# Values and gates of a gated recurrence as one block product in seven parts

## The chip, the cores and the metric

The kernel runs on one core of a Trainium2 chip. Its engines are named as in the profile: PE multiplies matrices (its weight loads are shown apart, as PEld), DVE, ACT and POOL do vector and scalar work, and SP only issues transfers. Times are microseconds of device time; a kernel's time is the median of its runs, and less is better. "Product" below means one matrix instruction of PE.

## The reference

One layer of a streaming encoder, in float32, for 512 tokens of width 1024. The change is in the combined input projection and in what follows from two of its eight outputs, `gi` (the recurrence's values) and `gg` (its gates):

```python
hn = rmsnorm(h, norm_mix_g[l])
proj = hn @ w_in[l]
fq, fk, fv, ff, gq, gf, gi, gg = jnp.split(proj, split_idx, axis=-1)
log_f = jax.nn.log_sigmoid((ff + fox_f_bias[l]).astype(jnp.float32)).transpose(0, 2, 1)
fox_out = fox_attention(to_heads(fq), to_heads(fk), to_heads(fv), log_f)
rec = hgrn2_chunkwise(gq, gf, gi, lbs[l])
rec = rmsnorm(rec, hgrn_norm_g[l]) * jax.nn.silu(gg...)
h = h + jnp.concatenate([fox_out, rec], axis=-1) @ w_out[l]
h = h + memory_cross_attention(rmsnorm(h, norm_x_g[l]), mem_n, ...)
h = h + jnp.square(jax.nn.relu(rmsnorm(h, norm_ff_g[l]) @ w1[l])) @ w2[l]
```

`w_in` has 3592 columns. `fv` is columns 1024 to 1535, `ff` 1536 to 1543, `gi` 2568 to 3079 and `gg` 3080 to 3591. `hgrn2_chunkwise` has 4 heads; in each chunk of 64 tokens its attention weights hold the product of the forget gates between two tokens, and a state of 128 x 128 per head goes from chunk to chunk.

## The kernel before, in words

**Products.** Every float32 operand is split into a high and a low part, and a matrix product is done as three: high by high, high by low, low by high. Tokens are contracted over 8 slices of 128 of the width; the scale of the norm (`r0`, one number per token) is applied to the result. `hn_hi` and `hn_lo` hold the transposed, gain-scaled input in its two parts; `x_T` makes them slice by slice, and `x_park` keeps the transposed input (`park`) and sends it to DRAM for the end of the layer.

**Weights.** They come as a stream of panels, in the order of the list `specs`. Each panel is two units (a and b, four slices of the width each, or two for wide panels of 512 columns). A unit is loaded by a transfer on SP into a `wr` tile (two buffers), ACT rounds it to its high part `wh` (L179), and DVE subtracts to get its low part `wl` (L183); four buffers hold the parts, two panels. `next_panel` hands out a panel and starts those up to two ahead, at a low priority. In this stretch the panels are: 0 and 1 the forget gates, 2 and 3 the queries of the recurrence (`gq`), 4 the first 256 columns of `gi` with the 8 of `ff`, 5 and 6 the two halves of the width for all of `gg`, 7 and 8 the same for the other 256 columns of `gi` with the first 256 of `fv`, and from 9 on the attention's queries and keys.

**The order.** PE's instructions run in the order in which the code writes them. The other engines' order is set by a scheduler from priorities. Between the steps of the recurrence the code puts products from a queue called `fill`: `fill.run(us)` takes products until their estimated time is used up, so PE has work while the vector engines do theirs.

**Levels.** The weights inside chunks are built in seven levels, m = 1, 2, 4 ... 64. A level is one set of products `lv` on PE from the tiles `mov` (keys and queries multiplied up) and `mix` (copies of them by ACT); DVE copies their results under a mask (L806); DVE and POOL multiply `mov` and `sta` by the gates' products `F` (DVE L825, POOL L826 for every other head), POOL multiplies `F` up (L828), ACT makes the next `mix`, and `fill.run(2 * F2)` follows. Level m = 64 instead puts its result into the tiles `A`. Then come the transposes of `A` (`pa`), the transposes of the keys (`pk`, copied by DVE to `kt` at L920), and the loop over the chunks with `po` and the state's product `pst` (L940), which reads `kt` and the values.

**Around it.** SP's queue also carries plain copies of MLP weights to DRAM (a table, `COPIES`, says how many after which load), on which POOL's accumulating transfers (L444) later add other blocks, at times given by `PACE`. The first row tile of the memory is loaded and normalised (L377 to L387) beside the keys.

Of the kernel before, what the change touches and what calls it, by code (L numbers as in the profile page):

```python
# [33 lines left out]
MT, NF = 3, 2  # L34
F1, F2, F3, F4, B1 = 1.6, 2.7, 1.5, 1.0, 2.0

# [4 lines left out]
RAWS, HB, LOADS = 5, 4, 8  # L41
COPIES = {7: 2, 16: 1, 17: 0, 21: 1}
PACE = (183.0, 4.7), (306.0, 11.5)


@with_exitstack
def emit(
# [141 lines left out]
    def load_unit(name, spec, ks, parts=1, between=None):  # L189
# [24 lines left out]
    def load_next(parts=2, between=None):  # L214

        i = len(stream)
        if i >= len(specs):
            return []
        units, splits = [], []
        uk = specs[i][0][1].shape[1] // 2  # L220
# [5 lines left out]
        stream.append(tuple([u[x] for u in units] for x in range(2)))  # L226
        return splits

    def next_panel():
# [179 lines left out]


    hn_hi, hn_lo = act_tile("hn_hi"), act_tile("hn_lo")
    xTd = drp.tile([4, P, 2, S], F32, name="xTd")
# [73 lines left out]
    presum.jobs.extend(j for _, j in sets)  # L486
    park = {}

# [18 lines left out]
    def x_park(c):  # L507
        part, new_ = c // 2, c // 2 not in park
        if new_:
            park[part] = s4([2, S], f"xT{part}")  # L510
        dst = park[part][:, c % 2, :]
# [4 lines left out]
        if not new_:  # L516
            gp.dma_start(xTd[part], park[part])

# [133 lines left out]
    gate(3)  # L652
    forget(3)
    for hp in range(2):
        wt = next_panel()
        for j in range(2):
            h = 2 * hp + j
# [32 lines left out]

    def proj_if():
        wt = next_panel()
        for tb in range(NT):
            ps = mm(f"gi0{tb}", (WT + FH,))
            yield from gemm_tm(ps, wt, hn_hi, hn_lo, tb)
            ac.activation(iv[tb // 2][:, tb % 2, 0:WT], ps[:, 0:WT], AF.Identity, scale=r0[:, tb : tb + 1])
            ve.scalar_tensor_tensor(z3[:, tb, :], ps[:, WT : WT + FH], r0[:, tb : tb + 1], fb, op0=ALU.mult, op1=ALU.add)
# [5 lines left out]

    fill.add(proj_if(), "ff")
    fill.add(new(gg, "gg"))
    fill.add(proj_wide([lambda tb: gg[tb // 2][:, tb % 2, :]], AF.Silu, "gg"), "gg")

# [4 lines left out]

    def proj_iv():
        yield from proj_wide([lambda tb: iv[tb // 2][:, tb % 2, WT:S], new_fv()], AF.Identity, "gi")

    fill.add(proj_iv(), "iv")

# [183 lines left out]

    mx_hi, mx_lo = act_tile("mx_hi"), act_tile("mx_lo")
    St = None
# [1015 lines left out]
```

## Time and profile before

| | |
|---|---|
| runs, us | 751.37, 751.83, 751.97 |
| median of the runs, us | 751.83 |
| the profiled execution, us | 751.99 |
| its span in the profile, us | 750.3 |
| mean granted clock of PE | 0.998 |
| bytes moved by transfers | 152.92 MB, 204 GB/s over the span |
| read from device memory, written | 147.91 MB, 51.40 MB |

The profile is of one execution. Rows that begin with a time are of the timeline: the start, how long, the engine, the code's line, the operation, what it writes and reads, the shape, and how many stand together; in brackets is how long the engine had been idle before and what it waited for last. Matrix instructions are pipelined and their ends are modelled, so starts are compared, not ends. Rows with a line first are groups: count, busy time and mean in ns, then idle time before them. Rows of transfers give their number, their size, and the median time from issue to landing.

### The profile page before, as it was taken

To read this page: it belongs to the slowest core of one execution; us is meant where nothing else is said; L and a number is where in the kernel's file an instruction comes from. 1 tells how busy PE (TensorE), PEld (TensorE's weight loads), DVE (VectorE), ACT (ScalarE), POOL (GpSimd) and SP (SyncE) were. 2 spreads that over 40 slices of the span, in tenths; PEclk is the share of its full clock that TensorE was granted. 3 is DMA by queue.
4 is the path that set the end of the run, shared out by engine and by line. 5 is a ranking of instruction groups with operands and counts; after the bars stand their busy time and mean duration, and the time that the engine had idled before them with its cause. 6 is when DMAs were issued, how large, how long until landed. Compare 5 with 4: busy or idle time off the path is not lost.

```text
span 750.3 us, 12293 instructions
## 1 busy us (share of the span) xinstructions
PE 742.9 (99%) x4581; PEld 649.6 (87%) x4581; DVE 546.5 (73%) x869; ACT 444.7 (59%) x749; POOL 202.1 (27%) x280
## 2 busy tenths in 40 slices
PE   9999999999999999999999999999999999999996
PEld 6889888888888888888888899898989899999985
DVE  5647873667878856645556898978787887878796
ACT  5655555556666742344434589666566757574864
POOL 7207531233433237621111212111111111100034
PEclk9999999999999999999999999999999999999999
DMA  8641987578957889985579799898989898978452
GB/s 250 200 116 58 298 262 228 172 231 269 289 187 224 265 225 210 193 165 122 121 165 197 114 250 238 237 226 247 230 218 235 220 247 214 240 198 232 133 113 113
DMA packets 109678, 152.92 MB, mean 204 GB/s; under 512 B 6145, under 2 KB 76074, under 8 KB 109618
## 3 DMA queue, kind: packets, MB, share of 16 engines
q1 hardware_dynamic: 85458, 112.52, 46.3%
q0 software_dynamic: 24000, 39.35, 30.1%
q8 instruction: 36, 0.59, 0.3%
q14 instruction: 24, 0.20, 0.1%
q10 hardware_dynamic: 160, 0.27, 0.1%
HBM read 147.91 MB, written 51.40 MB: 266 GB/s over the span
## 4 chain that ended last, share of the span: by engine, by line
PE 96%; DVE 1%; issue 1%; ACT 0%; POOL 0%; POOLq 0%; DVEq 0%
PE uU L1494 4%; PE uU L1496 4%; PE uU L1495 4%; PE U L1652 3%; PE U L1653 3%; PE U L1654 3%; PE uY L1495 2%; PE uY L1494 2%; PE uY L1496 2%; PE xk L1008 2%; PE xq L253 2%; PE wo L253 2%; PE xq L254 2%; PE xq L255 2%; PE xw L255 2%; PE xw L254 2%
## 5 line engine op out<-in xcount | busy, mean ns | idle before, releaser
L183 DVE TENSOR_TENSOR wlu<-wru,whu 128x1024 fp32r<-128x1024 f32 x53 | 64.2, 1225 | 28.0 <-ACT whu L179 27.9
L179 ACT ACTIVATE whu<-wru 128x1024 fp32r<-128x1024 f32 x53 | 55.9, 1058 | 43.7 <-PE U L1654 16.8
L183 DVE TENSOR_TENSOR wld<-wrd,whd 128x1024 fp32r<-128x1024 f32 x56 | 68.3, 1222 | 13.5 <-ACT whd L179 13.2
L179 ACT ACTIVATE whd<-wrd 128x1024 fp32r<-128x1024 f32 x56 | 59.0, 1053 | 12.6 <-PE uU L1495 5.2
L1652 PE MATMUL U<-whd,hb 128*128 128x512 f32 x120 | 46.8, 390 | 0.0
L1653 PE MATMUL U<-wld,hb 128*128 128x512 f32 x120 | 46.8, 390 | 0.0
L1654 PE MATMUL U<-whd,hb 128*128 128x512 f32 x120 | 46.7, 389 | 0.0
L1029 POOL TENSOR_SCALAR bi<-nF,Ft 128x128 f32<-128x128 f32 (+3 forms) x32 | 20.6, 652 | 59.8 <-PE pt L1065 38.8
L1494 PE MATMUL uU<-xs_hi,whu 128*128 128x256 f32 x128 | 36.3, 284 | 0.0
L1496 PE MATMUL uU<-xs_hi,wlu 128*128 128x256 f32 x128 | 36.2, 283 | 0.0
L1495 PE MATMUL uY<-xs_lo,whu 128*128 128x256 f32 x128 | 36.2, 283 | 0.0
L1494 PE MATMUL uY<-xs_hi,whu 128*128 128x256 f32 x128 | 36.2, 283 | 0.0
L1496 PE MATMUL uU<-x_hi,wlu 128*128 128x256 f32 x128 | 36.2, 283 | 0.0
L1496 PE MATMUL uY<-xs_hi,wlu 128*128 128x256 f32 x128 | 36.2, 283 | 0.0
L1495 PE MATMUL uU<-xs_lo,whu 128*128 128x256 f32 x128 | 36.2, 283 | 0.0
L1495 PE MATMUL uU<-x_lo,whu 128*128 128x256 f32 x128 | 36.2, 283 | 0.0
L1494 PE MATMUL uU<-x_hi,whu 128*128 128x256 f32 x128 | 36.2, 283 | 0.0
L444 POOL DMA_DIRECT2D wsd<-in_w_dram x16 | 17.9, 1116 | 63.6 <-PE xw L255 12.8
L1390 POOL DMA_DIRECT2D wrd<-in_w_dram x8 | 9.8, 1221 | 86.2 <-DVE wld L183 85.0
L444 POOL DMA_DIRECT2D wsu<-in_w_dram x14 | 17.1, 1218 | 48.9 <-PE xw L255 15.6
L1654 PEld LDWEIGHTS U<-whd,hb 128*128 128x128 f32 x120 | 22.5, 188 | 4.7
L1652 PEld LDWEIGHTS U<-whd,hb 128*128 128x128 f32 x120 | 22.6, 188 | 4.5
(944 smaller groups left out, 2605.2 us busy)
## 6 DMA issues: line engine op xcount, KB each, us to landing
wru<-in_w_dram SPq DMA_DIRECT2D x25, 512.0 KB, 7.9
wsd<-in_w_dram SPq DMA_DIRECT2D x24, 512.0 KB, 7.3
wrd<-in_w_dram SPq DMA_DIRECT2D x24, 512.0 KB, 4.3
wrd<-wsd SPq DMA_DIRECT2D x24, 512.0 KB, 4.9
wsu<-in_w_dram SPq DMA_DIRECT2D x21, 512.0 KB, 5.6
wru<-wsu SPq DMA_DIRECT2D x21, 512.0 KB, 6.1
wsd<-in_w_dram POOLq DMA_DIRECT2D x16, 512.0 KB, 7.8
wsu<-in_w_dram POOLq DMA_DIRECT2D x14, 512.0 KB, 6.9
```

The source lines that it names most:

```text
L179: at = ac.activation(hi, raw, AF.Copy)
L183: at_lo = ve.tensor_tensor(lo, raw, f(hi), ALU.subtract)
L253: te.matmul(ps, wh, hi, start=n_ == 0 and not begun, stop=False)
L254: te.matmul(ps, wh, lo, start=False, stop=False)
L255: at = te.matmul(ps, wl, hi, start=False, stop=k == order[-1])
L444: yield gp.dma_start(wsum[kind, g, name], src, accum_op=ALU.add, **more)
L1494: te.matmul(ps[:, i, :], whi[:, k, ws], xh[:, k, :], start=begin, stop=False, skip_group_check=True)
L1495: te.matmul(ps[:, i, :], whi[:, k, ws], xl[:, k, :], start=False, stop=False, skip_group_check=True)
L1496: at = te.matmul(ps[:, i, :], wlo[:, k, ws], xh[:, k, :], start=False, stop=k == UK - 1, skip_group_check=True)
L1652: te.matmul(ps, hi, whi[:, k, :], start=begin, stop=False, skip_group_check=True)
L1653: te.matmul(ps, hi, wlo[:, k, :], start=False, stop=False, skip_group_check=True)
L1654: at = te.matmul(ps, lo, whi[:, k, :], start=False, stop=k == 1, skip_group_check=True)
```

## The change

The values and the gates, 1024 columns in all, are computed together as one product of blocks, by a scheme that takes seven block products where the plain way takes eight. Width and columns are both halved: rows of the weight block are the halves of the width (0 and 1), its columns are `gi` (0) and `gg` (1), and tokens are halved too (two times 256). So a block product is 256 tokens by 512 of the width by 512 columns: 2 token tiles by 4 slices by 3, 24 products of PE with 512 columns. The order is the list `GORDER`.

- **Panels.** Panel 4 now has the first 256 columns of `fv` and the 8 of `ff`. Units 5 to 11 are the seven block products, each with halves a and b of two slices. What was panel 9 and on is 12 and on.
- **Weight sums.** With the blocks 00, 01, 10, 11: product 5 takes 00 + 01, product 6 takes 11 + 00 + 01, product 7 takes 01 + 11, product 4 takes product 6's sum + 10, and products 1, 3, 2 take 00, 11, 10 alone. A sum is a plain load by SP and an accumulating transfer by POOL on top of it (`accum_op`). Each has its function and its place: `early_sum` and `second_sum` around the panels of `gq`, `third_sum` (four transfers, one per slice, into four tiles) ahead of level m = 4, `fourth_sum` behind the splits of product 3. The split of products 7 takes its tiles slice by slice.
- **Token sums.** `park` stays in SBUF as one tile, is scaled by the norm's gain on ACT in place after its transfers to DRAM, and DVE forms four differences of its blocks (`hdif`); ACT and DVE split them into high and low parts in the tiles `mx_hi` and `mx_lo`, which later hold the mixer's output.
- **Results.** Products 1, 6, 7 and 4 accumulate in two banks (`gU`), 5, 3 and 2 in two others (`gW`). ACT scales a bank into a tile or copies it, DVE adds a bank to a tile. The sign of the gates is folded into `nr0`, the negative scale.
- **Constants.** `F2`, the fill per level, goes from 2.7 to 3.2; the table `COPIES` is shifted and `PACE` begins 5 us earlier on its own clock. Loads of the first four panels keep their written order on SP.

```diff
-F1, F2, F3, F4, B1 = 1.6, 2.7, 1.5, 1.0, 2.0
+F1, F2, F3, F4, B1 = 1.6, 3.2, 1.5, 1.0, 2.0
-COPIES = {7: 2, 16: 1, 17: 0, 21: 1}
-PACE = (183.0, 4.7), (306.0, 11.5)
+COPIES = {12: 2, 14: 3, 17: 2, 19: 1, 20: 0, 24: 1}
+PACE = (178.0, 4.7), (301.0, 11.5)
...
-    for n0 in (2056, 2312, 1544, 1800, 2568):
+    for n0 in (2056, 2312, 1544, 1800, 1024):
         specs.append(panel(w_in, n0))
-    specs += wide(w_in, 3080)
-    specs += wide(w_in, 2824, 1024)
+    GORDER = ("1", "5", "6", "3", "7", "2", "4")
+
+    def block0(rc):
+        r, c = int(rc[0]), int(rc[1])
+        return w_in[r * S : (r + 1) * S, 2568 + c * S : 2568 + (c + 1) * S].rearrange("(k p) n -> p k n", p=P)
+
+    specs += [lambda name=name: product_unit(name) for name in GORDER]
...
-                nc.sync.dma_start(raw_[:, qs, sl], src[:, src_ks, :])
+                dma = nc.sync.dma_start(raw_[:, qs, sl], src[:, src_ks, :])
+                if len(stream) == 4:
+                    tc.keep_in_program_order(dma)
...
+    def load_block(name, rc, tiles):
+        raw0[name] = tiles
+        for u, t in enumerate(tiles):
+            tc.keep_in_program_order(nc.sync.dma_start(t, block0(rc)[:, 2 * u : 2 * u + 2, :]))
+
+    def early_sum():
+        load_block("5", "00", [s4p.tile([P, 2, S], F32, tag="s4", name=f"wrs5{u}") for u in "ab"])
+        for u in range(2):
+            tc.keep_in_program_order(gp.dma_start(raw0["5"][u], block0("01")[:, 2 * u : 2 * u + 2, :], accum_op=ALU.add))
+
+    def second_sum():
+        t = t4("wrs6b").rearrange("p (k n) -> p k n", k=2)
+        load_block("6", "11", [s4p.tile([P, 2, S], F32, tag="s4", name="wrs6a"), t])
+        for u in range(2):
+            tc.keep_in_program_order(gp.dma_start(raw0["6"][u], raw0["5"][u], accum_op=ALU.add, max_dma_last_dim=2048))
+
+    def third_sum():
+        for k in range(4):
+            tc.keep_in_program_order(gp.dma_start(sums7[k], block0("11")[:, k, :], accum_op=ALU.add))
+
+    def fourth_sum():
+        for u in range(2):
+            tc.keep_in_program_order(gp.dma_start(raw0["6"][u], block0("10")[:, 2 * u : 2 * u + 2, :], accum_op=ALU.add))
+
+    def product_unit(name):
+        parts = [new_parts([2, S], f"{len(stream)}{u}") for u in "ab"]
+        stream.append(tuple([u[x] for u in parts] for x in range(2)))
+        if name in "13":
+            pad = [P, UK * UW]
+            tiles = [wrp.tile([P, 2 * S], F32, tag="wr", name=f"wr0{name}{u}", padded_shape=pad) for u in "ab"]
+            load_block(name, "00" if name == "1" else "11", [t.rearrange("p (k n) -> p k n", k=2) for t in tiles])
+        if name == "1":
+            for k in range(4):
+                t = q2p.tile([P, S], F32, tag="q2", name=f"wrs7{k}")
+                tc.keep_in_program_order(nc.sync.dma_start(t, block0("01")[:, k, :]))
+                sums7.append(t)
+        jobs = []
+        for u in range(2):
+            hi, lo = parts[u]
+            if name == "7":
+                jobs += [split_of(hi[:, k, :], lo[:, k, :], sums7[2 * u + k]) for k in range(2)]
+                continue
+            raw = raw0[{"2": "5", "4": "6"}.get(name, name)][u]
+            jobs.append(split_of(hi, lo, raw))
+        if name == "3":
+            jobs.append(fourth_sum)
+        if name == "3":
+            jobs.append(lambda: load_block("5", "10", raw0["5"]))
+        return jobs
...
+    def token_sums():
+        for c in range(KC):
+            ac.activation(park[:, c, :], park[:, c, :], AF.Identity, scale=g_mix[:, c : c + 1])
+        A1a, A2a, A1b, A2b = (park[:, ks, h] for ks in (slice(0, 4), slice(4, 8)) for h in (h1, h2))
+        for name in "5637":
+            hdif[name] = k4([4, WT], f"hd{name}")
+        ve.tensor_tensor(hdif["5"], A2b, A2a, ALU.subtract)
+        ve.tensor_tensor(hdif["6"], hdif["5"], A1a, ALU.add)
+        ve.tensor_tensor(hdif["3"], hdif["6"], A1b, ALU.subtract)
+        ve.tensor_tensor(hdif["7"], A1a, A2a, ALU.subtract)
+
+    def token_parts():
+        hs = [t.rearrange("p k (h n) -> p (k h) n", h=2) for t in (mx_hi, mx_lo)]
+        for i, name in enumerate("5637"):
+            hi, lo = hsum[name] = [t[:, 4 * i : 4 * i + 4, :] for t in hs]
+            sign = -1.0 if name == "6" else 1.0
+            ac.activation(hi, hdif[name], AF.Copy, scale=sign)
+            ve.scalar_tensor_tensor(lo, hdif[name], sign, f(hi), op0=ALU.mult, op1=ALU.subtract)
+        for name, ks, h in (("1", slice(0, 4), h1), ("2", slice(4, 8), h1), ("4", slice(4, 8), h2)):
+            hsum[name] = hn_hi[:, ks, h], hn_lo[:, ks, h]
+
     for hp in range(2):
         wt = next_panel()
+        if hp == 0:
+            early_sum()
+        if hp == 1:
+            second_sum()
+            token_sums()
+            mx_lo = act_tile("mx_lo")
+            token_parts()
...
+    def seven(names):
...
+        def done(name, t, ps):
+            if name == "1":
+                ac.activation(tok(iv, t), ps, AF.Identity, scale=r0[:, t : t + 1])
+            elif name == "2":
+                ve.scalar_tensor_tensor(tok(iv, t), ps, r0[:, t : t + 1], tok(iv, t), op0=ALU.mult, op1=ALU.add)
+            elif name == "4":
+                ac.activation(tok(iv, 2 + t), ps, AF.Identity, scale=r0[:, 2 + t : 3 + t])
+            elif name in "56":
+                ac.activation(tok(gg, t + (2 if name == "5" else 0)), ps, AF.Copy)
+            else:
+                tb = t + (2 if name == "7" else 0)
+                g_ = tok(gg, tb)
+                ve.tensor_tensor(g_, ps, g_, ALU.add)
+                ac.activation(g_, g_, AF.Silu, scale=nr0[:, tb : tb + 1])
...
+            pss = U if name in "1674" else W
+            whi, wlo = next_panel()
+            xh, xl = hsum[name]
+            for u in range(2):
+                for t, ps in enumerate(pss):
+                    ts_ = slice(t * P, (t + 1) * P)
+                    for kk in range(2):
+                        k = 2 * u + kk
+                        hi, lo, begin, end = xh[:, k, ts_], xl[:, k, ts_], name in "125" and k == 0, k == 3
+                        te.matmul(ps, hi, whi[u][:, kk, :], start=begin, stop=False, skip_group_check=True)
+                        te.matmul(ps, hi, wlo[u][:, kk, :], start=False, stop=False, skip_group_check=True)
+                        at = te.matmul(ps, lo, whi[u][:, kk, :], start=False, stop=end, skip_group_check=True)
+                        yield presum.tick(3 * S / 2400, at)
+                    if u == 1:
+                        done(name, t, ps)
+
+    fill.add(proj_ff(), "ff")
+    fill.add(new(gg, "gg"))
+    fill.add(seven(GORDER[:5]), "gg")
+    fill.add(seven(GORDER[5:]), "iv")
...
     for li, m in enumerate(mlev):
+        if li == 2:
+            third_sum()
```

Three places of the order, each before and after. In these rows stand the line, the operation, what is written and read, and the shape; DVE's and POOL's multiplications in one level are told apart by their shape.

DVE, in the recurrence, between its multiplications on `mov` at level m = 8 and those at m = 16 (`sta` and `mov` are the two operands, `wl` low parts of weight units, `wrs` tiles of weight sums, `gW` the second banks, `Ac` what a level writes). Before:

```order
L826 TENSOR_TENSOR sta_460<-sta_460,F_458 128x16x16
L825 TENSOR_TENSOR sta_460<-sta_460,F_458 128x16x16
L826 TENSOR_TENSOR sta_463<-sta_463,F_461 128x16x16
L825 TENSOR_TENSOR sta_463<-sta_463,F_461 128x16x16
L183 TENSOR_TENSOR wl8a<-wr8a,wh8a 128x1024
L806 COPY_PREDICATED Ac_656<-mku,lv_1113 128x8x16 x2
```

After:

```order
L188 TENSOR_TENSOR wl9b<-wrs_728,wh9b 128x512
L188 TENSOR_TENSOR wl9b<-wrs_730,wh9b 128x512
L963 TENSOR_TENSOR sta_458<-sta_458,F_456 128x16x16
L962 TENSOR_TENSOR sta_458<-sta_458,F_456 128x16x16
L963 TENSOR_TENSOR sta_461<-sta_461,F_459 128x16x16
L962 TENSOR_TENSOR sta_461<-sta_461,F_459 128x16x16
L188 TENSOR_TENSOR wl10a<-wrs5a,wh10a 128x1024
L824 TENSOR_TENSOR gg_916<-gW_992,gg_916 128x512
L824 TENSOR_TENSOR gg_916<-gW_993,gg_916 128x512
L188 TENSOR_TENSOR wl10b<-wrs5b,wh10b 128x1024
L943 COPY_PREDICATED Ac_693<-mku,lv_1215 128x8x16 x2
```

One split of a unit stood between the two levels; now there are two half splits, two whole ones, and two additions of a bank to the gates.

POOL, in the recurrence, between its multiplications of level m = 2 and those of m = 4 (`mov` and `F` as above, `wrs_7..` the four tiles of the third weight sum). Before:

```order
L826 TENSOR_TENSOR mov_459<-mov_459,F_458 128x128x2
L826 TENSOR_TENSOR mov_462<-mov_462,F_461 128x128x2
L828 TENSOR_TENSOR F_458<-F_458 128x256
L828 TENSOR_TENSOR F_461<-F_461 128x256
L826 TENSOR_TENSOR mov_459<-mov_459,F_458 128x64x4
L826 TENSOR_TENSOR mov_462<-mov_462,F_461 128x64x4
```

After:

```order
L963 TENSOR_TENSOR mov_457<-mov_457,F_456 128x128x2
L963 TENSOR_TENSOR mov_460<-mov_460,F_459 128x128x2
L965 TENSOR_TENSOR F_456<-F_456 128x256
L965 TENSOR_TENSOR F_459<-F_459 128x256
L258 DMA wrs_724<-in_w_in_dram 128x512
L258 DMA wrs_726<-in_w_in_dram 128x512
L258 DMA wrs_728<-in_w_in_dram 128x512
L258 DMA wrs_730<-in_w_in_dram 128x512
L963 TENSOR_TENSOR mov_457<-mov_457,F_456 128x64x4
L963 TENSOR_TENSOR mov_460<-mov_460,F_459 128x64x4
```

The four issues of the third sum now stand ahead of POOL's multiplications on `mov` for level m = 4.

DVE, behind the last level, from the last copies into `A` to the copy of the transposed keys (`A` and `kt` as above, `mov` the last multiplication, `m0m` and `mt` the norm of the memory's first row tile). Before:

```order
L819 COPY A_1300<-lv_1283 64x4x64
L820 COPY A_1300<-lv_1283 64x4x64
L825 TENSOR_TENSOR mov_462<-mov_462,F_461 128x4x64
L183 TENSOR_TENSOR wl9b<-wr9b,wh9b 128x1024
L183 TENSOR_TENSOR wl10a<-wr10a,wh10a 128x1024
L920 COPY kt_1408<-pk_1403 128x512
L385 TENSOR_TENSOR m0m<-m0m 128x1
L387 TENSOR_SCALAR mt_1388<-mt_1388,m0r 128x1024
```

After:

```order
L956 COPY A_1418<-lv_1401 64x4x64
L957 COPY A_1418<-lv_1401 64x4x64
L962 TENSOR_TENSOR mov_460<-mov_460,F_459 128x4x64
L188 TENSOR_TENSOR wl13a<-wr13a,wh13a 128x1024
L446 TENSOR_TENSOR m0m<-m0m 128x1
L448 TENSOR_SCALAR mt_1488<-mt_1488,m0r 128x1024
L188 TENSOR_TENSOR wl13b<-wr13b,wh13b 128x1024
L1056 COPY kt_1506<-pk_1501 128x512
```

The norm of the memory's row tile has come ahead of the copy to `kt`, and both splits of a unit pair stand around it.

More of the change, by code (lines that the diff above doesn't have):

```diff
@@ L218, in load_next @@
             return []
+        if callable(specs[i]):
+            return specs[i]()
         units, splits = [], []
@@ L408, in emit @@
     gp.affine_select(out=tri[:, 0, :], in_=tri[:, 0, :], compare_op=ALU.is_ge, fill=0.0, base=0, pattern=[[1, P]], channel_multiplier=-1)
+    park = ap_.tile([P, KC, S], F32, tag="act", name="park")
+    parked = set()
     hn_hi, hn_lo = act_tile("hn_hi"), act_tile("hn_lo")
@@ L486, in emit @@
     presum.jobs.extend(j for _, j in sets)
-    park = {}
     ms0 = sm(NT, "ms0")
@@ L507, in x_park @@
     def x_park(c):
[L508 to L511, printed above, removed]
+        part, dst = c // 2, park[:, c, :]
         if c % 2 == 0:
@@ L515, in x_park @@
             ve.tensor_copy(dst, xps[c])
-        if not new_:
-            gp.dma_start(xTd[part], park[part])
+        parked.add(c)
+        if c ^ 1 in parked:
+            gp.dma_start(xTd[part], park[:, 2 * part : 2 * part + 2, :])
     def x_sq(tb):
@@ L653, in emit @@
     forget(3)
+    mx_hi = act_tile("mx_hi")
+    nr0 = sm(NT, "nr0")
+    ve.tensor_scalar(nr0, r0, -1.0, None, op0=ALU.mult)
+    hsum, hdif = {}, {}
+    h1, h2 = slice(0, WT), slice(WT, S)
+    def token_sums():
[17 more added lines that the diff above has]
+            hsum[name] = hn_hi[:, ks, h], hn_lo[:, ks, h]
     for hp in range(2):
         wt = next_panel()
+        if hp == 0:
[5 more added lines that the diff above has]
+            token_parts()
         for j in range(2):
@@ L689, in emit, with proj_ff @@
     z3 = z.rearrange("p (t h) -> p t h", h=FH)
-    def proj_if():
+    def proj_ff():
         wt = next_panel()
+        dst = new_fv()
         for tb in range(NT):
@@ L702, in new @@
         yield
-    fill.add(proj_if(), "ff")
-    fill.add(new(gg, "gg"))
-    fill.add(proj_wide([lambda tb: gg[tb // 2][:, tb % 2, :]], AF.Silu, "gg"), "gg")
     def new_fv():
@@ L711, in new_fv, with tok @@
         return lambda tb, n0=0: t[:, tb, :]
-    def proj_iv():
-        yield from proj_wide([lambda tb: iv[tb // 2][:, tb % 2, WT:S], new_fv()], AF.Identity, "gi")
-    fill.add(proj_iv(), "iv")
+    U, W = [], []
+    def seven(names):
+        def tok(ts, tb):
+            return ts[tb // 2][:, tb % 2, :]
+        def done(name, t, ps):
[12 more added lines that the diff above has]
+                ac.activation(g_, g_, AF.Silu, scale=nr0[:, tb : tb + 1])
+        for name in names:
+            if name == "1":
+                U.extend(mm(f"gU{t}") for t in range(2))
+            elif name == "5":
+                W.extend((mm("gW0"), pvt("gW1")))
+            pss = U if name in "1674" else W
[17 more added lines that the diff above has]
+    fill.add(seven(GORDER[5:]), "iv")
     Ac = []
```

4 lines of the change are left out of this document (2 added, 2 removed).

## The prediction

> **What bounds the kernel now.** I read the page first: its span, its share of busy time by engine, the granted clock and the chain of work that ended last.
>
> ```profile
> span 750.3 us, 12293 instructions
> PE 742.9 (99%) x4581; PEld 649.6 (87%) x4581; DVE 546.5 (73%) x869; ACT 444.7 (59%) x749; POOL 202.1 (27%) x280
> PEclk9999999999999999999999999999999999999999
> PE 96%; DVE 1%; issue 1%; ACT 0%; POOL 0%; POOLq 0%; DVEq 0%
> ```
>
> The chain is PE for 96% of the span, at full clock in every slice. But a busy PE can hide slack, since ends of matmuls are modelled, so I went to the timeline of PE inside the stretch that the change rewrites and compared starts, not ends. Below are the first and the last of the 24 products of one half unit (tile 8a) and the transpose behind them.
>
> ```profile
> 112.85 0.39 PE L281 MATMUL gi<-wh8a,hn_hi 128*128 128x512 f32 x1
> ...
> 118.06 0.39 PE L283 MATMUL gi<-wh8a,hn_lo 128*128 128x512 f32 x1
> 118.29 0.49 PE L878 MATMUL pa<-ident,A 128*128 128x128 f32 x3
> ```
>
> From 112.85 to 118.29 there are 24 products of 512 columns in 5.44 us: one starts every 0.227 us, with no hole. PE is the bound here because its queue never runs dry, and a product less is 0.227 us less as long as that stays so. The question is therefore whether the others still keep ahead of it. Next come two levels of the recurrence, and the busy time of all engines in the two stretches that the change touches (columns: PE, PEld, DVE, ACT, POOL, then clock, DMA share, GB/s).
>
> ```profile
> 72.47 1.16 PE L800 MATMUL lv<-mov,mix 128*64 128x64 f32 x32
> 79.92 1.15 PE L800 MATMUL lv<-mov,mix 128*64 128x64 f32 x32
> 35.00:65.00 30.00, 30.00 (x214) 25.91 (x213) 15.48 (x19) 17.09 (x27) 6.23 (x4) 1.00 0.43 120
> 65.00:125.00 60.00, 60.00 (x461) 50.24 (x460) 39.38 (x86) 32.72 (x59) 25.43 (x36) 1.00 0.73 230
> ```
>
> A level with 27 products took 7.45 us; DVE is busy 39.4 of the 60 us of the levels, ACT 32.7.
>
> **The products removed.** Before, values, gates and half of the attention's values are one 264-column panel and two times 96 products of 512 columns, 192 in all. Now the panel has its own 256 columns changed for others, and values and gates are seven block products of 24, so 168. That is 24 products less: 24 x 0.227 = 5.45 us. The level matmuls, transposes and everything behind keep their number.
>
> **More fill per level.** F2 puts 30 products into a level (33 once) where 24 or 27 stood. With 7.45 us for 27, a level of 30 lasts 7.45 + 3 x 0.227 = 8.1 us, one of 33 8.8. This takes nothing away by itself: from the first level to the first state product (pst) both orders hold 192 such products, so pst stays at 126.0 us if PE never waits, and the 24 missing ones are gained behind it, where the attention's own products now start earlier.
>
> **Vector work in the levels.** This is where a stall would come from. Rows for the prices: a half split of 512 columns, an addition read from PSUM, the first and last instruction of the levels m = 2 and m = 32, and a split of 1024.
>
> ```profile
> 14.80 0.68 DVE L183 TENSOR_TENSOR wl0b<-wr0b,wh0b 128x512 fp32r<-128x512 f32 x1
> 55.71 0.69 DVE L660 TENSOR_TENSOR sta<-gq,rbc 128x512 f32<-128x512 f32 x1 [0.63 <-PE gq L255]
> 76.04 0.74 DVE L806 COPY_PREDICATED Ac<-mku,lv 128x128 f32<-128x128 uint8 x2
> 79.51 0.41 DVE L825 TENSOR_TENSOR sta<-sta,F 128x256 f32<-128x256 f32 x1
> 101.94 0.50 DVE L806 COPY_PREDICATED Ac<-mku,lv 128x128 f32<-128x128 uint8 x2 [0.43 <-PE lv L800]
> 104.92 0.41 DVE L825 TENSOR_TENSOR sta<-sta,F 128x256 f32<-128x256 f32 x1
> 106.45 1.23 DVE L183 TENSOR_TENSOR wl9a<-wr9a,wh9a 128x1024 fp32r<-128x1024 f32 x1 [1.12 <-ACT wh9a L179]
> ```
>
> A level's own vector work takes 79.92 - 76.04 = 3.9 us early and 105.33 - 101.94 = 3.4 us late; I take 3.9 for m = 2 and 4, 3.4 for 8, 16 and 32. The new order adds per level: m = 2 three splits and the small gate sums (3.7 + 0.8), m = 4 one split and two halves (1.2 + 1.4), m = 8 two halves, two splits and two gate additions (1.4 + 2.5 + 1.4), m = 16 two splits and two additions (2.5 + 1.4, and 0.2), m = 32 two splits, two value additions and a copy (2.5 + 1.4 + 0.7). With the base: 8.4, 6.5, 8.7, 7.5 and 8.0, together 39.1 us, against 8.1, 8.1, 8.8, 8.1 and 8.1 = 41.2 of PE. It fits, at 95%, without a single in-order wait counted. What saves it is depth: a level's multiplications on mov are due only at the next level, 30 products (6.8 us) later, and take some 2.5 us, so DVE may lag by about 4 us before PE feels it. I cost it at nothing; the cover is that lag, and each microsecond beyond it is one of PE.
>
> **The token sums, early.** Eight scalings of park (0.6 us each) and four high halves (1.05) go to ACT, four subtractions and four low halves to DVE: 8 x 1.23 = 9.8 us ahead of the panel's split wl4a.
>
> ```profile
> 45.44 1.25 DVE L183 TENSOR_TENSOR wl4a<-wr4a,wh4a 128x1056 fp32r<-128x1056 f32 x1
> 56.69 0.39 PE L266 MATMUL gi<-wh4a,hn_hi 128*128 128x264 f32 x1
> ```
>
> That split ended at 46.7 and PE wants it at 56.7. DVE idles half of 35 to 65 (15.5 of 30 busy), so roughly half of the 9.8 is absorbed: wl4a ends near 52, with 4 us left, and near 56.5 if nothing is absorbed. Zero on the path.
>
> **The four sums.** Ten accumulating transfers are issued on POOL, and their plain loads on SP ahead of the copies for the MLP's sums. Sums 5 and 6 are issued while POOL idles before its first level work. The third (four issues) stands between POOL's F of m = 2 and its mov of m = 4, the fourth one level later.
>
> ```profile
> 78.20 0.78 POOL L828 TENSOR_TENSOR F<-F 128x256 f32<-128x256 f32 x1 [0.34 <-DVE mov L825]
> 80.76 2.40 POOL L826 TENSOR_TENSOR mov<-mov,F 128x256 f32<-128x256 f32 x2 [1.79 <-PE lv L800]
> L444 POOL DMA_DIRECT2D wsd<-in_w_dram x16 | 17.9, 1116 | 63.6 <-PE xw L255 12.8 <-PE uY L1496 11.8 <-PE U L1654 11.3
> wsd<-in_w_dram POOLq DMA_DIRECT2D x16, 512.0 KB, 7.8
> wru<-in_w_dram POOLq DMA_DIRECT2D x7, 512.0 KB, 10.9
> ```
>
> An accumulating issue of twice the size holds POOL 1.12 us. From 79.0, four of them end at 83.5, then mov takes 2.4, so 85.9. Level m = 2 moves to 72.47 + 6 x 0.227 = 73.8, m = 4 to 82.0, m = 8 to 90.1: POOL is 4.2 us early, and an issue would have to cost (90.1 - 79.0 - 2.4) / 4 = 2.2 us to be felt. The landing: 83.5 + 10.9 = 94.4 at the worst median, while PE starts on that unit (9a) 24 products into the level m = 8, at 90.1 + 1.3 + 5.4 = 96.8, and with its second half 2.7 later; the first two of the four land a microsecond or two sooner. Sum 4, issued near 88 and landed by 99, is wanted at 110. Zero again.
>
> The trace does have something that speaks against these prices: work of POOL and DVE that overlaps gets longer. The same multiplication of two heads, beside the splits of two levels and alone at the end, and a split beside POOL's work:
>
> ```profile
> 73.31 3.53 POOL L826 TENSOR_TENSOR mov<-mov,F 128x256 f32<-128x256 f32 x2 [1.64 <-PE lv L800]
> 110.78 1.21 POOL L826 TENSOR_TENSOR mov<-mov,F 128x256 f32<-128x256 f32 x2
> 56.93 1.88 DVE L183 TENSOR_TENSOR wl5b<-wr5b,wh5b 128x1024 fp32r<-128x1024 f32 x1
> ```
>
> 3.53 against 1.21 is a factor of 2.9, 1.88 against 1.23 one of 1.5. That 1.12 us is a mean over 16 issues in a kernel whose DVE is 73% busy, so I keep it; an issue stretched 2.9 times, 3.3 us, is the other bound and goes to the rivals.
>
> [...]
>
> **The end of the stretch.** Here the order puts new things ahead of a copy that PE waits for: DVE's copy of the transposed keys (kt), wanted by pst.
>
> ```profile
> 112.75 0.43 DVE L820 COPY A<-lv 64x256 f32<-64x256 f32 x1
> 121.87 0.69 DVE L920 COPY kt<-pk 128x512 f32<-128x512 f32 x1 [1.07 <-PE pk L917]
> 127.18 0.75 DVE L387 TENSOR_SCALAR mt<-mt,m0r 128x1024 f32<-128x1024 f32 x1 [0.97 <-POOL m0r L377]
> 126.02 1.06 PE L940 MATMUL pst<-iv,kt 128*128 128x128 f32 x8
> ```
>
> Before, kt was done at 122.6, 3.4 us ahead. Now the last level starts 10.2 us ahead of pst, at 115.8 (fewer products lie between), and was at 109.0; the copies to A ended 4.2 us behind it, so 120.0. Then come wl13a (1.23), the memory row's norm (0.2, a wait of 1.0 for POOL, 0.75), wl13b (1.23) and kt (0.69): 125.1. The margin falls to 0.9 us. A lag of DVE of 2 us, or a late landing of the unit that wl13b splits, turns it into a wait of 1 to 2 us. I take 0.4 us, and keep 0 and 2.0 for the range.
>
> **Sum.** -5.45 + 0.4 = -5.05. The profiled run took 751.99 us (750.3 of span and 1.7 around it): 746.9. The median of the three runs is 0.16 lower: **746.8 us**. Its own range: 745.8 (no wait at kt, and the 0.6 us by which the three runs differ) to 749.0 (2.0 us at pst, 0.6 elsewhere).
>
> **Rivals.** (1) DVE becomes the bound of the levels, and the kernel gets slower. In the old levels a split starts only after a wait for its high half from ACT:
>
> ```profile
> 87.67 1.58 DVE L183 TENSOR_TENSOR wl7b<-wr7b,wh7b 128x1024 fp32r<-128x1024 f32 x1 [1.43 <-ACT wh7b L179]
> ```
>
> If each of the ten full splits in the five levels keeps such a wait, DVE needs 39.1 + 14.3 = 53.4 us against 41.2; less the 4 us of lag, PE loses 8.2: 746.8 + 8.2 = 755.0. It decides from a DVE total of about 50 us on (5.05 of gain and 4 of lag over 41.2). Against it: those waits stood where DVE had nothing due, and ACT has 27 us free of the 60 us. (2) Issues hold POOL at 2.9 times their price: from 79.0, four of 3.3 us end at 92.1, mov at 94.5, which m = 8 wanted at 90.1. That is 4.4 us of wait and 751.2, no change. For it: the stretched multiplications; against it: 1.12 us measured under load. (3) The margin at kt is gone wholly: DVE comes 2 to 3 us late through the last levels, and A, kt and the state steps behind wait: some 3 us more, 749.8. (4) The 24 products were hidden anyway: then 751.8; the holeless starts speak against it.
>
> **Chances.** Forecast 0.60, (3) 0.14, (2) and (4) together 0.08, (1) 0.18. No change is within 0.2%, 1.5 us, about what a measurement of this kernel can tell: faster is below 750.3, so 0.60 + 0.14 = 0.74, same 0.08, slower 0.18. Range 745.0 to 752.4: below, 0.8 us more of the 7.4 that PE idles in its span (750.3 - 742.9) may go with the new order; above, (4) with the 0.6 us between runs. It leaves out (1) and little else.
>
> **What would show it.** In the changed profile: seven groups of 24 products at a pitch of about 0.23 and no start more than 0.3 us late at the levels m = 4, 8 and 16; pst near 126; POOL's third sum issued near 79 to 84 at about 1 us each; wl13a, mt, wl13b and kt back to back on DVE. Level periods well above 8.1 to 8.8 us with DVE near full show rival (1); a late POOL mov at m = 8 shows (2); pst beyond 128 shows (3). I am wrong if PE waits more than 3 us in 56 to 130 us. The copies for the MLP begin some 10 us later than before, and could make a weight load late behind 130 us; the tightest unit there is this one:
>
> ```profile
> 230.73 1.23 DVE L183 TENSOR_TENSOR wl18b<-wr18b,wh18b 128x1024 fp32r<-128x1024 f32 x1 [0.54 <-ACT wh18b L179]
> 237.47 0.40 PE L1008 MATMUL xk<-me,wh18b 128*128 128x512 f32 x1
> ```
>
> It is split 5.5 us ahead of its use (237.47 - 231.96), so a load that is late by more than that would cost what is beyond it.

## The result, and the profile after

| | before | after |
|---|---|---|
| median of 6 runs, us | 751.75 | 756.0 |
| lowest and highest | 751.37, 751.97 | 754.02, 756.84 |
| ratio, 95% interval | | 1.0052 (1.0038 to 1.0066) |
| the profiled execution, us | 751.99 | 754.02 |
| its span, us | 750.3 | 752.2 |

The kernel became slower by half a per cent, where 0.7% faster was forecast. The profiled execution is the shortest of the six; a second one, below, has the same shape.

The page of the changed kernel: its span, the busy time of the engines, the granted clock in 40 slices, and the chain that ended last.

```profile
span 752.2 us, 12313 instructions
PE 740.2 (98%) x4557; PEld 646.4 (86%) x4557; DVE 565.5 (75%) x892; ACT 460.4 (61%) x769; POOL 212.5 (28%) x290
PEclk9999999989999999999999999999999999999999
PE 88%; DMA 4%; ACT 3%; DVE 2%; issue 1%; POOL 1%; POOLq 0%; DVEq 0%; SPq 0%; ACTq 0%
```

24 matrix instructions are gone (4557 against 4581) and PE is busy 2.7 us less, yet the span grew. A slice of the clock has fallen, and the chain is no longer PE alone: transfers, ACT and DVE stand in it with 9%. PE's starts in the changed stretch (the levels m = 2, 4 and 64, and the first state product), then the busy time of all engines there:

```profile
73.91 1.16 PE L937 MATMUL lv<-mov,mix 128*64 128x64 f32 x32
82.02 1.15 PE L937 MATMUL lv<-mov,mix 128*64 128x64 f32 x32
115.87 1.95 PE L937 MATMUL lv<-mov,mix 128*128 128x128 f32 x16
126.24 1.06 PE L1076 MATMUL pst<-iv,kt 128*128 128x128 f32 x8
```

```profile
65.00:125.00 60.00, 59.92 (x458) 49.84 (x457) 53.86 (x107) 43.76 (x76) 31.99 (x44) 1.00 0.73 199
```

The forecast had 73.8, 82.0, 115.8 and 126.0. DVE went from 39.4 to 53.9 us of 60 and PE did not wait for it. The loss is elsewhere. PE's waits from 35 to 190 us (line, what it waited for, total, times, longest), the stretch behind the first attention pair, and the clock around it (columns as before: the sixth number behind the stretch's length, its counts in brackets left out, is the granted clock):

```profile
PE pt L1201 <- DVE bi L1189: 4.3, 2, 4.0
```

```profile
163.41 0.45 PE L1201 MATMUL pt<-ident,bi 128*128 128x128 f32 x1 [3.98 <-DVE bi L1189]
164.14 0.45 PE L1201 MATMUL pt<-ident,bi 128*128 128x128 f32 x1 [0.29 <-DVE bi L1189]
...
166.09 0.41 PE L327 MATMUL fv<-wh14b,hn_hi 128*128 128x256 f32 x1
166.31 0.41 PE L328 MATMUL fv<-wl14b,hn_hi 128*128 128x256 f32 x1
```

```profile
155.00:160.00 5.00, 4.43 (x37) 4.22 (x36) 3.31 (x4) 0.00 (x0) 4.38 (x9) 1.00 0.00 0
160.00:165.00 5.00, 1.30 (x5) 1.07 (x6) 4.28 (x12) 1.36 (x5) 0.00 (x0) 0.64 0.60 156
165.00:170.00 5.00, 5.00 (x32) 5.00 (x31) 3.95 (x13) 4.60 (x13) 0.00 (x0) 0.67 1.06 383
```

PE reached the first transpose of the attention weights (`pt`) at 159.4, 4.2 us before the old kernel did (163.60), and then stood idle for 4.0 us and 0.3 us. Some 0.7 of these 4.2 us are luck: in this execution PE had its first products with the weights that much earlier, at 6.12 and not 6.84 us. Before and after:

```profile
6.84 0.81 PE L545 MATMUL gf<-hn_hi,wh0a 128*128 128x512 f32 x2
```

```profile
6.12 0.73 PE L605 MATMUL gf<-hn_hi,wh0a 128*128 128x512 f32 x2
```

Behind the wait PE ran slowly: until about 168 us products of 256 columns started 0.213 us apart at a granted clock of 0.50, against 0.12 at 1.00 in the kernel before; from 169 us on the clock is back at 1.00.

What was late? The same places in the kernel before, first on DVE and PE, then on POOL (`nF` is a bias row of the attention, loaded by POOL from the DRAM copy of the gates' sums; `bi` the bias and then the weights; `m1r` the scale of the memory's second row tile; `mt` that tile):

```profile
155.53 1.10 DVE L387 TENSOR_SCALAR mt<-mt,m1r 128x1024 f32<-128x1024 f32 x1 [2.37 <-POOL m1r L377]
163.17 0.29 DVE L1053 TENSOR_SCALAR bi<-bi,dn 128x128 f32<-128x128 f32 x1
163.60 0.70 PE L1065 MATMUL pt<-ident,bi 128*128 128x128 f32 x2
```

```profile
143.56 1.16 POOL L889 DMA_DIRECT2D nF<-Fd  x2
150.86 1.03 POOL L377 TENSOR_TENSOR hr<-hr3e,mhalf 128x4 f32<-128x4 f32 x1
151.90 0.73 POOL L1029 TENSOR_SCALAR bi<-nF,Ft 128x128 f32<-128x128 f32 x2
154.93 0.56 POOL L377 TENSOR_TENSOR m1r<-m1re,mhalf 128x1 f32<-128x1 f32 x1
```

There `bi` was done at 163.46 and PE came at 163.60: a margin of 0.14 us that no wait shows. And in the changed kernel, POOL and then DVE:

```profile
144.96 1.16 POOL L1026 DMA_DIRECT2D nF<-Fd  x2
147.08 1.03 POOL L438 TENSOR_TENSOR hr<-hr3e,mhalf 128x4 f32<-128x4 f32 x1
152.64 0.38 POOL L1165 TENSOR_SCALAR bi<-nF,Ft 128x128 f32<-128x128 f32 x1 [4.53 <-DMA nF<-Fd]
156.01 0.55 POOL L438 TENSOR_TENSOR m1r<-m1re,mhalf 128x1 f32<-128x1 f32 x1
```

```profile
156.60 1.09 DVE L448 TENSOR_SCALAR mt<-mt,m1r 128x1024 f32<-128x1024 f32 x1 [6.00 <-POOL m1r L438]
162.97 0.28 DVE L1189 TENSOR_SCALAR bi<-bi,dn 128x128 f32<-128x128 f32 x1
```

The last chunk's `hr`, which depends on PE, came 3.8 us earlier, as it should. But POOL then waited 4.5 us for `nF`, whose issue came 1.4 us later than before, and which took 7.6 us to land and not 4.0 (median of its two transfers):

```profile
nF<-Fd POOLq DMA_DIRECT2D x2, 256.0 KB, 4.0
```

```profile
nF<-Fd POOLq DMA_DIRECT2D x2, 256.0 KB, 7.6
```

The issue came later because it stands behind the third chunk's `hr` (142.59 before, 143.99 after), and that waits for ACT's sums `hj`; in ACT's order two `q` stood ahead of these before, and four `kh` stand there now. Before and after:

```profile
139.65 1.28 ACT L851 ACTIVATE q<-qk 64x512 fp32r<-64x512 f32 x2 [3.27 <-DVE qk L848]
140.96 0.28 ACT L957 ACTIVATE hj<-po 128x128 f32<-128x128 f32 x1
```

```profile
139.81 0.63 ACT L1001 ACTIVATE kh<-qk 64x512 fp32r<-64x512 f32 x1 [2.13 <-DVE qk L997]
142.31 0.25 ACT L1093 ACTIVATE hj<-po 128x128 f32<-128x128 f32 x1
```

Behind `nF` in POOL's order stands `m1r`; behind `m1r` in DVE's order stand `mt`, the query's low parts, a weight split and the softmax, with a second weight split inside it. So a late bias row is a late memory norm, a late softmax and a late `pt`. The transfers among which `nF` ran, in 140 to 145 us, before and after (last two columns: share of the transfer engines, GB/s):

```profile
140.00:145.00 5.00, 5.00 (x26) 4.12 (x24) 3.87 (x11) 3.56 (x12) 2.57 (x5) 1.00 0.02 7
```

```profile
140.00:145.00 5.00, 4.96 (x32) 4.07 (x31) 3.31 (x7) 4.05 (x13) 1.21 (x3) 1.00 1.09 374
```

They went from idle to full: `COPIES` now lays three plain MLP copies at each half of the panels 14 to 16, where the old table had two from panel 7 on. Without these copies (first experiment below) the same stretch moved 105 GB/s.

### The profile page after: what moved, and what is told of

Read it like the earlier page. It is cut to its first block, busy times and chain, and to the rows that moved or that the text cites. A ratio compares the mean times of both kernels' runs of the same rounds, so it can differ in the third digit from the quotient of the medians.

```text
span 752.2 us, 12313 instructions
## 1 busy us (share of the span) xinstructions
PE 740.2 (98%) x4557; PEld 646.4 (86%) x4557; DVE 565.5 (75%) x892; ACT 460.4 (61%) x769; POOL 212.5 (28%) x290
## 4 chain that ended last, share of the span: by engine, by line
PE 88%; DMA 4%; ACT 3%; DVE 2%; issue 1%; POOL 1%; POOLq 0%; DVEq 0%; SPq 0%; ACTq 0%
PE uU L1630 4%; PE uU L1632 4%; PE uU L1631 4%; PE U L1789 4%; PE U L1788 4%; PE U L1790 4%; PE uY L1632 2%; PE uY L1631 2%; PE uY L1630 2%; PE xk L1144 2%; PE xq L314 2%; PE wo L314 2%; PE xq L315 2%; PE xw L314 2%; PE xq L316 2%; PE xw L316 2%
## 5 line engine op out<-in xcount | busy, mean ns | idle before, releaser
L1790 PE MATMUL U<-whd,hb 128*128 128x512 f32 x120 | 46.7, 389 | 0.0
L1187 ACT ACTIVATE bi<-bi,mx 128x128 f32<-128x128 f32 (+3 forms) x32 | 17.9, 559 | 18.4 <-DVE mx L1185 17.4
L1790 PEld LDWEIGHTS U<-whd,hb 128*128 128x128 f32 x120 | 22.5, 188 | 4.7
```

The costliest lines, as they stand in the source:

```text
L1790: at = te.matmul(ps, lo, whi[:, k, :], start=False, stop=k == 1, skip_group_check=True)
```

## The experiments

Theory A: the products are saved as forecast, and the loss is one wait, from `nF` by way of `m1r`, with the low clock behind it. Rival B: the softmax's own vector work sets `pt` near 163 us whatever the transfers do.

**Copies moved away from nF.**

```diff
-COPIES = {12: 2, 14: 3, 17: 2, 19: 1, 20: 0, 24: 1}
+COPIES = {12: 2, 14: 0, 17: 4, 19: 1, 20: 0, 24: 1}
```

> The changed kernel, with the plain copies for the MLP taken out of the loads of panels 14 to 16 (3 per half panel become 0; panels 17 and 18 carry 4 in place of 2, the rest is made up where the sums need it). Theory A (the gain in products is there, but the bias rows nF of the first attention pair land late because these copies now fill the transfer engines; POOL waits for them ahead of the memory norm's m1r, DVE waits for m1r ahead of the softmax, and PE waits 4.3 us for the transpose pt and then runs at a lower clock): nF lands 4 to 5 us after its issue and not 7.6, pt starts at 159.3 to 160.5 and not 163.4, PE waits under 1.2 us, no slice of the clock below 0.95, 747 to 749 us. Theory B (the vector engines' own work for the softmax sets pt near 163 whatever the transfers do): pt at 162.5 or later, 754 to 757 us.

Measured: 758.18 us, ratio 1.0093 (1.0078 to 1.0108), slower still. The expected step was there, smaller than thought, and another loss came with it, so that the time is 9 us above the upper end of the expected range. PE's rows at `pt`, and its waits from 190 to 250 us:

```profile
160.72 0.30 PE L1201 MATMUL pt<-ident,bi 128*128 128x128 f32 x1 [1.29 <-DVE bi L1189]
161.46 0.30 PE L1201 MATMUL pt<-ident,bi 128*128 128x128 f32 x1 [0.43 <-DVE bi L1189]
```

```profile
PE pv L1217 <- ACT pts L1205: 1.5, 1, 1.5
PE pv L1217 <- DVE pts L1207: 1.5, 1, 1.5
PE pt L1201 <- DVE bi L1189: 1.1, 1, 1.1
PE pt L1201 <- DVE dn L1188: 0.5, 1, 0.5
```

`pt` came 2.7 us earlier, so B falls in its plain form; but 1.7 us of wait were left, and the clock fell behind them all the same (0.62 from 161 to 165 us). The copies only moved: with four at each half of panels 17 and 18, ACT waited 2.5 us for a weight load among them (`wr18a`) and 5.4 us for the next panel's (`wr19a`), and PE was busy 55.4 of the 60 us from 190 to 250.

**The bias rows issued early, copies as they are.** `NF` is the chunk behind which the rows are issued.

```diff
-MT, NF = 3, 2
+MT, NF = 3, 0
```

> The changed kernel, with the two transfers of the bias rows nF issued on POOL behind the first chunk's hr (near 131 us) and not the third's (145 us); copies as in the changed kernel. Theory A: nF has landed by 142, POOL's biases start behind the last chunk's hr at 148.1, m1r at 151 to 152, pt at 159.3 or under 0.5 us later, no drop of the clock, 746.5 to 748 us. Theory B: pt stays near 163, 754 to 757 us. If the copies hurt by another way than nF (the weight unit 15), 752 us or more.

Measured: 747.98 us, ratio 0.9951 (0.9935 to 0.9968). POOL's biases and PE's transposes:

```profile
148.36 0.75 POOL L1165 TENSOR_SCALAR bi<-nF,Ft 128x128 f32<-128x128 f32 x2
```

```profile
159.50 0.38 PE L1201 MATMUL pt<-ident,bi 128*128 128x128 f32 x2
```

No wait at `pt`, the clock full (1.00 from 130 to 190 us). The rows now took 9.6 us to land among the same copies, which harms nothing, since they are issued 14 us earlier. One number of the kernel turns 0.5% slower into 0.5% faster.

**More products ahead of the transpose.**

```diff
-FX = (4.4, 4.4, 5.4, 5.4), (3.3, 3.9, 4.5, 5.1)
+FX = (8.8, 4.4, 3.2, 3.2), (3.3, 3.9, 4.5, 5.1)
```

> The changed kernel, with 8.8 us of other products between the first scores and their transpose in place of 4.4, and 3.2 in place of 5.4 in the third and fourth steps. nF stays late. Theory A: pt starts near 163.7 without a wait, the clock stays at full, and both the 4.3 us and the 2 us of slow products behind them are won back: 748 to 751 us (the poorer third and fourth steps may cost up to 2). If the low clock behind 160 us does not come from PE's idling, the slice 165 to 170 stays at 0.67 and the time at 751 to 753.

Measured: 752.59 us, ratio 1.0017 (1.0008 to 1.0027). `pt` started at 164.3 without a wait and the clock stayed at 1.00, as expected; the poorer steps behind it then cost more than the 2 us allowed (PE busy 8.17 of 10 us from 180 to 190), and the time is 1.6 us above the expected range.

**The second norm moved behind the softmax.**

```diff
         mt.append(m_)
+        if t == 0:
+            norm_rows(m_, f"m{t}")
...
             fox_scores(*pairs[n])
+            if n == 0:
+                norm_rows(mt[1], "m1")
```

> The changed kernel, with the norm of the second memory tile (ACT's squares, m1r on POOL, mt on DVE) moved behind the first softmax; nF and the copies as in the changed kernel, so nF still lands near 153. If the late rows hurt by way of m1r and DVE's order (theory A), pt starts at 158.5 to 160 although nF is as late as before; then mt is late instead and PE waits 1 to 3 us at the memory's transpose mnt: 748 to 752 us. If the late rows hurt straight through the biases, pt stays above 162 and the time at 754 or more.

Measured: 748.88 us, ratio 0.9963 (0.995 to 0.9976). POOL waited for `nF` about as long as in the changed kernel (4.3 and 4.5 us), and `pt` was on time:

```profile
152.65 0.48 POOL L1166 TENSOR_SCALAR bi<-nF,Ft 128x128 f32<-128x128 f32 x1 [4.28 <-DMA nF<-Fd]
```

```profile
159.49 0.38 PE L1202 MATMUL pt<-ident,bi 128*128 128x128 f32 x2
159.71 0.27 PE L1119 MATMUL mnt<-ident,mt 128*128 128x128 f32 x1
160.71 0.55 PE L1119 MATMUL mnt<-ident,mt 128*128 128x128 f32 x3 [0.73 <-DVE mt L448]
```

So the late rows hurt only through the order: `m1r` on POOL, `mt` on DVE ahead of the softmax.

**Both moves** (the two diffs above together).

> The changed kernel with both moves of the last two kernels: the bias rows nF issued behind the first chunk's hr, and the second memory tile's norm behind the first softmax. If late rows, through m1r, are the one cause (theory A), each move alone takes it away and both together bring little more: 747 to 748.5 us, no wait at pt, under 1 us at mnt. If they are two causes that add, 744 to 745.5 us.

Measured: 749.66 us, ratio 0.9971 (0.996 to 0.9982), 1.2 us above the upper end. They do not add, which speaks for one cause. `pt` did not wait, and `mnt` waited 0.7 us. Both together are even slower than either alone (747.98 and 748.88); why is not known.

**Copies thinned without crowding others.**

```diff
-COPIES = {12: 2, 14: 3, 17: 2, 19: 1, 20: 0, 24: 1}
+COPIES = {12: 2, 14: 1, 17: 2, 20: 1}
```

> The changed kernel with the copies thinned in the loads of panels 14 to 16 (1 per half panel and not 3) without crowding panels 17 and 18 (2 as before), the rest carried one by one from panel 20 on. Theory A: nF lands 4 to 5.5 us after its issue, pt starts at 159.5 to 161, and the 4 to 5 us that the kernel with no copies lost at 190 to 250 us do not come (its panels 17 and 18 carried 4): 748 to 751 us. If those 4 to 5 us belonged to the changed kernel itself, 753 or more.

Measured: 751.98 us (750.59 to 754.73 in ten runs), ratio 1.001 (0.9998 to 1.0022), 4 us better than the changed kernel's first median (3 than its second, below), 1 us above what was expected. Its profiled execution, 754.52 us, is one of the slowest of the ten. In it `nF` landed about 5 us after its issue, yet a wait of 1.3 and 0.4 us was left at `pt`, as in the first experiment. So of the 4.3 us some 2.6 go with the copies; 1.7 stay, and I put them down to the issue, which stands on POOL behind the third chunk's `hr` and came 1.4 us later, not earlier with PE. The kernel with early rows moves that issue and loses both parts; the two were not separated further.

**A control: both moves in the kernel before the change.**

> A control: the kernel before the change, with the same two moves (rows nF behind the first chunk's hr, the second memory tile's norm behind the first softmax). Theory A: there PE arrived at pt just as the softmax was done, so there is nothing to win: 751.2 to 752.0 us. If the two moves are a gain of their own, 748 to 750 us, and what they gave to the changed kernel says nothing on the change.

Measured: 750.94 us, ratio 0.9993 (0.9983 to 1.0002), 0.3 us below the expected range and no change within its interval. The moves gain little without the missing products.

**The old fill per level, rows early.**

```diff
-F1, F2, F3, F4, B1 = 1.6, 3.2, 1.5, 1.0, 2.0
+F1, F2, F3, F4, B1 = 1.6, 2.7, 1.5, 1.0, 2.0
...
-MT, NF = 3, 2
+MT, NF = 3, 0
```

> The changed kernel with the rows nF early, and with the old fill per level (2.7 and not 3.2), so levels hold 24 or 27 products. Five levels then last about 37 us on PE, and DVE has 39 us of work in them. If the additional fill is needed for the vector work (the prediction's sum), PE waits 1 to 3 us in the levels m = 4 to 32: 749 to 751.5 us. If DVE's lag of some 4 us covers it, 747.5 to 748.5 us, as with the new fill.

Measured: 754.14 us, ratio 1.0036 (1.0023 to 1.0049): 6.2 us worse than with the new fill, for a reason that was not expected. The levels kept their pace (no wait at any `lv`); PE stopped behind them, and its clock fell to 0.75 from 125 to 130 us. Here are its wait and what ACT did meanwhile:

```profile
126.38 0.33 PE L1053 MATMUL pk<-ident,sta 128*128 128x128 f32 x1 [3.69 <-ACT A L1016]
```

```profile
124.79 1.06 ACT L184 ACTIVATE wh13a<-wr13a 128x1024 fp32r<-128x1024 f32 x1 [5.99 <-DMA wr13a<-in_w_in_dram]
125.75 0.58 ACT L1016 ACTIVATE A<-pa 128x512 f32<-128x512 f32 x1
```

ACT stood 6.0 us at the split of a weight unit that had not landed, with the copy of `A` queued behind it. So the larger fill is needed, but not for DVE: neither of the two expectations held. That it is there to give the loads time is how I read these rows; it was not tried alone.

**Products written over, to keep PE busy in the wait.** 18 products of 512 columns, whose results are not used, stand ahead of the first `pt`.

```diff
         pt = tr(f"pt{h}{tb}")
+        for i in range(18 if u == (0, 0, 0) else 0):
+            te.matmul(pt, hn_hi[:, i % KC, 0:P], hn_hi[:, i % KC, :], start=True, stop=True)
```

> The changed kernel with 18 products of 512 columns (4.1 us) put into PE's queue just ahead of the first transpose pt, their result written over: pure heating of the 4.3 us in which PE waited. If the low clock behind the wait comes from the wait (theory A), pt still starts at 163.3 to 164, the clock stays full behind it and the time falls by the 2 us of slow products: 753.5 to 754.5 us against 756.0. If the low clock comes from something else near 160 us (the transfers, the other engines' load), the slice 165 to 170 stays near 0.67 and the time at 756 or above.

Measured: 753.27 us (752.08 to 754.19 in ten runs), ratio 1.0018 (1.0009 to 1.0028), 0.2 us below the expected range, 2.7 us below the changed kernel's first median and 1.8 below its second (755.11, next experiment), which ran beside it. `pt` was even later than expected (164.72), and the clock stayed full (1.00 in each 5 us from 150 to 180):

```profile
160.22 4.27 PE L1200 MATMUL pt<-hn_hi 128*128 128x512 f32 x18
164.72 0.33 PE L1203 MATMUL pt<-ident,bi 128*128 128x128 f32 x1 [0.23 <-DVE bi L1189]
```

So the low clock came with the wait (0.67 from 165 to 170 us in the changed kernel, 1.00 here), and cost about 2 us on top of it.

**The changed kernel once more.**

> The changed kernel itself once more, for a second trace of it: its runs lay between 754.0 and 756.8 us and the trace of the first is of the shortest. If the spread is the same wait with other lengths (theory A: the landing of nF, and how long the clock stays low), this trace shows nothing longer anywhere else, and pt at 163 to 166; if there is another loss, it shows at another place of PE's queue.

Measured: 755.11 us, ratio 1.0045 (1.003 to 1.006), trace of 753.2 us. PE's first products with the weights came at 6.99 us, 0.9 later than in the first trace, and the levels (74.74 for m = 2) and `pst` (127.11) as much later. The wait is the same (3.9 and 0.3 us at `pt`, which started at 164.14) and no other of PE is longer than 0.5; the span's last microsecond more lies behind the last MLP products (first `wo` at 270.6 against 270.5, the last `U` at 739.8 against 739.7).

**Rows early, and fill moved to where a wait of 0.95 us was left.**

```diff
-FX = (4.4, 4.4, 5.4, 5.4), (3.3, 3.9, 4.5, 5.1)
+FX = (4.4, 4.4, 5.4, 5.4), (3.3, 4.9, 4.5, 4.1)
...
-MT, NF = 3, 2
+MT, NF = 3, 0
```

> The changed kernel with the rows nF early, and 1 us of fill moved from the fourth to the second step of the later attention pairs, where the kernel with early rows still waited 0.95 us at a pt near 221 us. If that wait was plain lack of fill, 747.0 to 747.8 us; if the fourth step then lacks it, 748 to 749 us.

Measured: 748.12 us, ratio 0.9948 (0.9932 to 0.9965): the wait was gone from the trace, and the time the same as with the rows early alone: it lies in the second expected range, but no wait in the fourth step shows. This kernel and the one with the rows early alone are the fastest tried; the late norm, alone or with them, also beats both kernels.

## Why the prediction was wrong, point by point

- **The bound and the products removed: right.** PE reached `pt` 4.2 us earlier (3.5 counted from its first product with the weights), and in the kernel with early rows the memory's first product came at 184.4 us against 189.5: 5.1 of the 5.45 us (4.9 counted so).
- **Fill, levels, DVE's total: right.** DVE worked 39.8 of the 42.0 us from m = 2 to m = 64 (forecast 39.1), PE did not wait, and rivals (1) and (3) fell. The four level starts that the prediction gives were met within 0.1 us, but by luck: without the early start of this execution they would be 0.8 us late, and in the second trace m = 2 came 0.9 late. The sum of 41.2 us for the five levels was 0.8 short and did not fit the prediction's own 115.8: the levels m = 16 and 32 took 8.5 us and not 8.1, since the small products `pF` and `pFr` stand in them.
- **The third sum: right.** POOL issued it from 80.28 us, and `mov` was done at 85.3 (forecast 85.9, wanted at 90.1). Rival (2) did not come: four issues took 3.6 us in all, where it had four of 3.3 us.
- **The token sums: perhaps mis-sized.** They were put at nothing on the path, but the last `dg` and the first level were 0.7 us late (18.97 us from the first `dg` to m = 2, where 16.87 and six products of 0.227 make 18.23). DVE split `wl4a` up to 53.1 us, where 46.7 had been before, and the next units came late with it; that this is the token sums' doing was not tried alone.
- **The copy to kt: right.** Forecast to end at 125.1, it ended at 124.9, and `pst` started at 126.24, 0.2 us behind the forecast; 0.4 had been allowed. Here too the early start helped: from the first product with the weights to `pst` both traces of the changed kernel took 120.1 us, where it was 119.2 before, so 0.9 us was lost on the way.
- **The step that failed** is the sentence "the 24 missing ones are gained behind it, where the attention's own products now start earlier". It took for granted that the vector engines there would come earlier too, and put nothing on the path for them. The rows of before showed that they had 0.14 us to spare at `pt`, and the prediction did not compare them: a page with PE at 99% and no waits was read as slack of the others. The last part saw that the copies would begin later, and asked only whether a weight load would be late (5.5 us of slack); the transfer that was late is a bias row of 256 KB that POOL issues. Through `m1r` and `mt` it held the softmax, and `pt` started at 163.4 and not at 159.4; with the rows early or the norm late it starts at 159.5. The price: 4.3 us of wait and about 2 us of low clock. With the 0.9 us lost ahead of `pst` and the 5.45 us gained that is 1.8 us slower; the profiled execution was 2.0 us slower, with its early start.
- What stays open: the difference of 2 us between the median, 4.25 us slower than before, and the profiled execution. A second trace shows 1 us of it at the end of the kernel, none at `pt`.

## What to carry to other kernels

A gain on the bounding engine reaches the end only as far as the next meeting point at which the others also come earlier: compare, in the trace of before, when an operand is ready and when the bound takes it, at each such point behind the edit, not only inside it. When a table of background transfers is shifted, every small load in its new stretch belongs on the list, and what is queued behind its reader. Here POOL's wait for `nF` (4.5 us, with `m1r` behind it in POOL's order) was best removed by issuing the load earlier: one number, worth 8 us against the changed kernel's first median and 7 against its second. And a start that meets its forecast within 0.1 us proves little where two traces of one kernel differ by 0.9 us from their first products on.

## What the runs showed of the hardware

The low clock came with short waits, but the length of a wait alone did not decide it. With 1.29 and 0.43 us of idle within 2 us (copies moved away) PE's clock was 0.62 in the next 4 us; with 1.33 and 0.43 us (copies thinned) it was 0.65 from 163 to 167 us. With single waits of 0.73 us (norm late) and 0.95 us (rows early) it stayed at 1.00; behind one of 1.13 us (copies moved away, at 199 us) products of 512 columns started 0.23 us apart, as ahead of it. The clock was also 1.00, from 180 to 190 us, with 0.47 and 1.36 us within 2.5 us (more products ahead of the transpose):

```profile
184.83 0.63 PE L1201 MATMUL pt<-ident,bi 128*128 128x128 f32 x4 [0.47 <-DVE bi L1189]
186.82 0.63 PE L1201 MATMUL pt<-ident,bi 128*128 128x128 f32 x4 [1.36 <-DVE bi L1189]
```

What else decides is not shown here. Slow products of 256 columns started 0.213 us apart at a granted clock of 0.50 (the changed kernel, 165 to 168 us), against 0.12 at 1.00.
